# Layer 0's attention in 64-row score matmuls and split transposes, with the forget terms added by VectorE

## The chip, the cores and the metric

One core of a Trainium2 chip runs the whole program in one launch. The metric is the device time of an execution in microseconds, the median over the runs. The profile is that of one execution.

## The reference

Two decoder layers over 2048 positions of width 1024, batch 1. Each layer norms its input, scales and shifts it by a conditioning vector, mixes over positions and adds the gated, normed result.

Layer 0's mixer has two parts over one projection:

- FoX, 8 heads of 64: scores q.k/8 + (F[query] - F[key]) under the causal mask, where F is the running sum of log-forget gates of the head; softmax; times v; divided by the sum; gated by SiLU. F[query] is the same for all keys of a row and leaves the softmax as it is.
- Differential attention, 4 heads: two causal score maps with their own queries and keys of 64, two softmaxes p1 and p2, and (p1 - lam p2) v with v of 128 columns; then an RMSNorm and the gate.

Layer 1's mixer (dilated windows, 16 heads) is not touched but for where the code of its transposes stands.

All is float32 outside; scores are multiplied in parts, a high and a low one, in the type fp32r, as qh.kh + qh.kl + ql.kh.

## The kernel before

The stages follow each other: projections of layer 0 (to about 790 us), its attention (791 to 1600), its output projection, then the same for layer 1. A scheduler orders each engine's instructions by the order in which the program names them, the buffers at hand and its own estimate of costs.

`attention0` runs over pairs p of heads: 0 to 3 are four pairs of FoX heads, 4 to 7 the four differential heads with their two maps. Each p has two halves of eight units. A unit is a block of 128 queries, number i, against its i + 1 blocks of 128 keys. Half 0 alternates units of chunk 3 (i 12 to 15) and chunk 0 (i 0 to 3); half 1 those of chunk 2 and chunk 1. `run` takes the units in order. A unit's scores are put, piece by piece, into the groups of the unit three before it (AHEAD = 3).

- `scores`, one head (or map) at a time: for each piece of up to 512 keys two matmuls of 128 contraction rows into one bank of the tile `s` (three banks). Rows 0 to 63 and 64 to 127 of the key and query tiles hold different parts, so two matmuls give the three products; FoX's forget terms ride along as four extra rows (K1, K2, Q1, Q2 tiles, filled once with ones and zeros). DVE evicts each bank (L845, L848 with the causal mask `maskd` for the last piece) and takes the row minimum of the negated scores; ACT then does the exponential over the row in place (L853) and its sum.
- `combine` (differential only): DVE multiplies P1 by c1 and adds P0 (L883 to L885).
- `turn`, per group of 4 key blocks: `flip` transposes the blocks of 128 by 128 on TensorE (L701) into one bank of `t` (two banks) and copies it out as a tile `pt` (L704). FoX: ACT and DVE by turns; differential: ACT.
- `av`, one group later: probabilities times values into `o` (L919), FoX in 64-column halves for its two heads.
- `finish`: the divisors, for the differential heads the norm (L964 to L970; the product with the gate, L969, on POOL).

POOL is otherwise idle in this stage. Loads go through the SP queue, those before the first unit through POOL's. The last key tiles become room for the output weights: `WO_AT` says at which units six of eight are loaded, the other two are loaded in `out_proj`.

Layer 1's stage `dilated` has its two heads side by side in 64 rows each (L1256, three products), and transposes in two parts of 64 rows (L1283, copied out in L1288, its AV is L1305).

Of the kernel before, what the change touches and what calls it, by code (L numbers as in the profile page):

```python
# [8 lines left out]
F32 = mybir.dt.float32  # L9
F32R = mybir.dt.float32r  # L10
# [8 lines left out]
S, D = 2048, 1024  # L19
# [63 lines left out]
def trunk(ctx: ExitStack, tc: tile.TileContext, A, out):  # L83
# [42 lines left out]
    f_d = dram.tile([4, 8, S], F32R, name="fd")  # L126
# [376 lines left out]
    def forget():  # L503
# [27 lines left out]
        fh = fp.tile([128, 128], F32R, name="fh")  # L531
        fl = fp.tile([128, 128], F32R, name="fl")
        SC.copy(fh, ps[:, 256:384])
        V.tensor_tensor(fl, ps[:, 256:384], fh.bitcast(F32), OP.subtract)
        for part, x in ((0, fh), (1, fl)):
            dma(dap(f_d, part * 8 * S, [[128, 128], [1, 128]]), x)
            n = fp.tile([128, 128], F32R, name=f"fn{part}")
            V.tensor_scalar(n, x.bitcast(F32), -1.0, None, OP.mult)
            dma(dap(f_d, (2 + part) * 8 * S, [[128, 128], [1, 128]]), n)
# [87 lines left out]
    def first_rows(l, wo, ps_p, og, gh, gl, more=None):  # L627
# [8 lines left out]
        for e in range(len(wo)) if more is None else range(7):  # L636
            if more is not None:
                more(e)
# [58 lines left out]
    def flip(ap, aps, blocks, eng, bufs):  # L697

        ps = aps.tile([128, 512], F32, tag="t", name="t_ps", bufs=2)
        for j, b in enumerate(blocks):  # L700
            TE.transpose(ps[:, 128 * j:128 * j + 128], b, ident)  # L701
        n = 128 * len(blocks)
        pt = ap.tile([128, 512], F32, tag="pt", name="pt", bufs=bufs)
        last_flip[eng is SC] = SC.copy(pt[:, :n], ps[:, :n]) if eng is SC else V.tensor_copy(pt[:, :n], ps[:, :n])  # L704
        return pt
# [18 lines left out]
    P_BUFS = ((512, 4), (1024, 4), (2048, 4))  # L724
    HALVES = ((3, 0), (2, 1))

    def attention0():
# [8 lines left out]
        aps = pool(aps_es, "atps", 1, PS)  # L736

        def k_tile(j, n):
            K = kp.tile([128, S], F32R, name=f"K{n}_{j}")
            if n == 2:  # L740
                PO.memset(K[64:128, :].bitcast(F32), 1.0)
            return K

        Ks = [k_tile(j, n) for j in range(2) for n in (1, 2)]
        Q2s = [ap.tile([128, 512], F32R, name=f"Q2_{j}") for j in range(8)]

        def q_fill(eng, js):
            for j in js:
                eng.memset(Q2s[j][64:128, :].bitcast(F32), 0.0)
                eng.memset(Q2s[j][64:68, :].bitcast(F32), 1.0)  # L750

        q_fill(V, range(4))
        Q1s = [ap.tile([128, 512], F32R, name=f"Q1_{j}") for j in range(8)]
        M = 16 * 64 * S
        keys, queries, values, gates = {}, {}, {}, {}

        def load_k(p, j):
            h = 2 * (p % 4) + j
            if p >= 4:
                K = Ks[(h + 4) % 6]  # L760
                for a in (0, 1024):
                    dma2(K[:, a:a + 1024], qkd, (8 + h) * 64 * S + a, M, [[S, 64], [1, 1024]])
                keys[p, j] = K, K
                return
            K1, K2 = Ks[2 * (h % 3):2 * (h % 3) + 2]
            o = 64 * j * S
            for a in (0, 1024):
                dma2(K1[:, a:a + 1024], qk0[4 + p], o + a, 128 * S, [[S, 64], [1, 1024]])
                dma(K2[0:64, a:a + 1024], dap(qk0[4 + p], o + a, [[S, 64], [1, 1024]]))
                dma(K2[66:68, a:a + 1024], dap(f_d, h * S + a, [[8 * S, 2], [1, 1024]]))  # L770
            keys[p, j] = K1, K2

        def load_q(p, half, ns=(0, 1)):
            for n in ns:
                c = HALVES[half][n]
                for j in range(2):
                    h = 2 * (p % 4) + j
                    s = 4 * half + 2 * n + j
                    Q1, Q2 = Q1s[s], Q2s[s]
                    a = 512 * c  # L780
                    if p >= 4:
                        dma2(Q1, qkd, h * 64 * S + a, 0, [[S, 64], [1, 512]])
                        last = dma2(Q2, qkd, M + h * 64 * S + a, 0, [[S, 64], [1, 512]])
                    else:
                        o = 64 * j * S + a
                        dma2(Q1, qk0[p], o, 0, [[S, 64], [1, 512]])
                        dma(Q2[0:64], dap(qk0[p], 128 * S + o, [[S, 64], [1, 512]]))
                        last = dma(Q2[64:66], dap(f_d, (16 + h) * S + a, [[8 * S, 2], [1, 512]]))
                    queries[p, j, c] = Q1, Q2
            return last  # L790
# [9 lines left out]
        def loads_at(p, half):  # L800

            if half == 0:
                if 0 < p < 4:
                    load_k(p, 1)
                if p < 7:
                    load_k(p + 1, 0)
                if 3 <= p < 7:
                    load_k(p + 1, 1)
                load_q(p, 1)
            elif p < 7:  # L810
                load_q(p + 1, 0)
# [3 lines left out]
        load_k(0, 0)  # L815
        load_q(0, 0, (0,))
        dma(maskd, A["cst"][:, C_MD:C_MD + 512])
        load_k(0, 1)
# [3 lines left out]
        with tc.issue_after(last.ins):  # L822
            q_fill(PO, range(4, 8))
            Ks += [k_tile(2, n) for n in (1, 2)]
            rw = row_tiles(ap2, 2)

        def scores(d, j, p, i, l):
# [4 lines left out]
            m4 = ap.tile([128, 8], F32, tag="m4", name="m4", bufs=16)  # L832

            def piece(k):
                if k == 0:
                    d[j] = ap.tile([128, n0], F32, tag=f"P{n0}", name=f"P{n0}", bufs=bufs)
                P = d[j]
                c0, n = cl[k]
                ps = aps.tile([128, 512], F32, tag="s", name="s_ps", bufs=3)
                for a in range(2):  # L840
                    TE.matmul(ps[:, :n], queries[p, j, i // 4][a][:, 128 * (i % 4):128 * (i % 4) + 128],  # L841
                              keys[p, j][a][:, c0:c0 + n], start=a == 0, stop=a == 1)
                m = m4[:, k:k + 1]
                if k < len(cl) - 1:
                    V.tensor_scalar(P[:, c0:c0 + n], ps[:, :n], 0.0, 3.0e38, OP.add, OP.min, accum_out=m)  # L845
                    return
                u = min(n, W - c0)
                V.tensor_tensor_reduce(P[:, c0:c0 + u], ps[:, :u], maskd[:, 512 - u:512], 1.0, 3.0e38,  # L848
                                       OP.add, OP.min, m)
                if len(cl) > 1:  # L850
                    m = m4[:, 4:5]
# [608 lines left out]
```

## Time and profile before

| what | value |
|---|---|
| median of 3 runs | 3265.45 us (3259.69 to 3265.56) |
| the profiled execution | 3263.24 us, span 3261.5 us |
| TensorE matmul busy | 3149.6 us (97%), granted clock 0.982 |
| DVE, ACT, POOL busy | 1572.2, 1294.9, 427.8 us (48, 40, 13%) |
| layer 0's attention, FoX pairs | about 791 to 1250 us |
| layer 0's attention, differential heads | about 1250 to 1600 us |

Matmuls overlap, so a busy time near 100% does not say how much of it could go; the distance from one start to the next does. Times in a stage are to be read from that stage's windows, not from the page's totals.

### The profile page before, as it was taken

Reading aid. Unit: us, or ns where it says so; the run is one execution under the profiler, and the core shown is the slowest. Engines: PE = TensorE matmul, PEld = TensorE weight load, DVE = VectorE, ACT = ScalarE, POOL = GpSimd, SP = SyncE. Lnnn points to the kernel's source line nnn. Section 1 sums busy time; section 2 is a strip of 40 time slices with the busy share of each in tenths; the row PEclk is TensorE's granted clock in tenths of the full one; section 3 lists DMA queues with packets and bytes.
Section 4 is the critical chain, followed back from the end, with each engine's and each line's share of the span. In section 5 each row is a group of like instructions: output and inputs, shape, how many; then the busy total and the mean of one; then the engine's idle time right before and its main releaser. Section 6 shows DMA issues by size and latency. Waiting matters only on the chain. (4 is left out here: it accounts for less than half of the span.)

```text
span 3261.5 us, 56531 instructions
## 1 busy us (share of the span) xinstructions
PE 3149.6 (97%) x22044; PEld 2603.7 (80%) x22044; DVE 1572.2 (48%) x4180; ACT 1294.9 (40%) x2937; POOL 427.8 (13%) x404
## 2 busy tenths in 40 slices
PE   7999999999999999999999999999999899989898
PEld 6978889987777778888778998888888777767687
DVE  6443421002666668888663402311100677777743
ACT  5311111112555556777542321111111767676321
POOL 3200100003000000010032202220000022212422
PEclk8999999999999999999999999999999999998899
DMA  7255542217223324432342324674314554544252
GB/s 261 80 183 189 175 144 85 72 62 194 69 78 98 93 66 125 117 92 72 120 159 104 132 86 134 201 217 142 113 62 148 161 169 158 179 153 143 79 191 97
DMA packets 281812, 424.12 MB, mean 130 GB/s; under 512 B 32156, under 2 KB 160156, under 8 KB 276552
## 3 DMA queue, kind: packets, MB, share of 16 engines
q1 hardware_dynamic: 277496, 407.87, 40.1%
q0 software_dynamic: 4048, 12.64, 1.4%
q8 instruction: 173, 2.83, 0.4%
q14 instruction: 95, 0.78, 0.1%
HBM read 268.15 MB, written 152.25 MB: 129 GB/s over the span
## 5 line engine op out<-in xcount | busy, mean ns | idle before, releaser
L245 PE MATMUL pj<-hl,wh 128*128 128x512 f32 x1536 | 389.1, 395 | 0.0
L245 PE MATMUL pj<-hh,wh 128*128 128x512 f32 x1536 | 389.1, 395 | 0.0
L245 PE MATMUL pj<-hh,wl 128*128 128x512 f32 x1536 | 388.9, 395 | 0.0
L841 PE MATMUL s_ps<-K,Q 128*128 128x512 f32 (+2 forms) x1280 | 356.4, 391 | 8.6 <-DVE P L845 8.1
L245 PEld LDWEIGHTS pj<-hl,wh 128*128 128x128 f32 x1536 | 289.1, 188 | 68.9 <-issue 0.5
L245 PEld LDWEIGHTS pj<-hh,wl 128*128 128x128 f32 x1536 | 288.6, 188 | 68.3 <-issue 0.2
L853 ACT ACTIVATE P<-P,m 128x1664 f32<-128x1664 f32 (+15 forms) x256 | 307.2, 1201 | 89.9 <-DVE m L852 84.0
L245 PEld LDWEIGHTS pj<-hh,wh 128*128 128x128 f32 x1536 | 287.9, 188 | 68.3 <-issue 1.0
L919 PE MATMUL o_ps<-pt,v 128*64 128x128 f32 (+1 forms) x3264 | 335.6, 281 | 6.3 <-ACT pt L704 5.5
L919 PEld LDWEIGHTS o_ps<-pt,v 128*64 128x64 f32 (+1 forms) x3264 | 271.2, 155 | 69.3 <-issue 43.1
L1266 ACT ACTIVATE P<-P,st 128x256 f32<-128x256 f32 (+3 forms) x512 | 266.8, 523 | 107.5 <-DVE st L1264 106.7
L230 DVE TENSOR_TENSOR wl<-w,wh 128x512 fp32r<-128x512 f32 (+1 forms) x128 | 84.9, 705 | 404.9 <-ACT wh L229 404.9
L845 DVE TENSOR_SCALAR_CACHE_REDUCE P<-s_ps 128x512 f32<-128x512 f32 (+1 forms) x384 | 248.4, 667 | 64.8 <-PE s_ps L841 58.9
L701 PE MATMUL t_ps<-cc,P 128*128 128x128 f32 x1632 | 251.3, 278 | 4.0 <-DVE c L884 1.6
L1264 DVE CUSTOM_DVE_ANT_0 P<-s_ps,band 128x256 f32<-128x256 f32 (+3 forms) x512 | 204.2, 446 | 99.7 <-PE s_ps L1256 94.5
L841 PEld LDWEIGHTS s_ps<-K,Q 128*128 128x128 f32 x1280 | 209.0, 190 | 48.1 <-DVE P L845 16.7
L704 ACT COPY pt<-t_ps 128x512 f32<-128x512 f32 (+3 forms) x320 | 163.4, 517 | 197.9 <-PE t_ps L701 195.9
L1256 PE MATMUL s_ps<-K,Q 64*128 64x256 f32 (+2 forms) x1536 | 202.3, 334 | 24.7 <-DVE st L1264 23.3
L701 PEld LDWEIGHTS t_ps<-cc,P 128*128 128x128 f32 x1632 | 187.3, 142 | 39.1 <-issue 25.8
L266 ACT ACTIVATE hi<-pj 128x512 fp32r<-128x512 f32 x80 | 47.9, 598 | 348.7 <-PE pj L245 309.5
L1305 PE MATMUL o_ps<-pt,v 128*64 128x128 f32 x2272 | 179.6, 291 | 5.4 <-DMA v<-v 5.4
L1256 PEld LDWEIGHTS s_ps<-K,Q 64*128 64x128 f32 x1536 | 147.3, 197 | 46.1 <-DVE st L1264 34.9
(247 smaller groups left out, 4584.9 us busy)
## 6 DMA issues: line engine op xcount, KB each, us to landing
Q<-q SPq DMA_DIRECT2D x31, 1024.0 KB
ada<-ada_w SPq DMA_DIRECT2D x96, 256.0 KB
sg<-t2k SPq DMA_DIRECT2D x64, 256.0 KB
Q<-qkd SPq DMA_DIRECT2D x128, 128.0 KB
w<-w SPq DMA_DIRECT2D x64, 256.0 KB
xt<-x SPq DMA_DIRECT2D x32, 512.0 KB
q<-yb SPq DMA_DIRECT2D x64, 256.0 KB
x<-x SPq DMA_DIRECT2D x28, 512.0 KB
```

The source lines that it names most:

```text
L230: V.tensor_tensor(wl[:, 2 * q:2 * q + 2, :n], w[:, :, :n], wh[:, 2 * q:2 * q + 2, :n].bitcast(F32), OP.subtract)
L245: TE.matmul(ps, a[:, d, 128 * j:128 * j + 128], b[:, d, :], start=n == 0, stop=n == 23)
L701: TE.transpose(ps[:, 128 * j:128 * j + 128], b, ident)
L704: last_flip[eng is SC] = SC.copy(pt[:, :n], ps[:, :n]) if eng is SC else V.tensor_copy(pt[:, :n], ps[:, :n])
L841: TE.matmul(ps[:, :n], queries[p, j, i // 4][a][:, 128 * (i % 4):128 * (i % 4) + 128], keys[p, j][a][:, c0:c0 + n], start=a == 0, stop=a == 1)
L845: V.tensor_scalar(P[:, c0:c0 + n], ps[:, :n], 0.0, 3.0e38, OP.add, OP.min, accum_out=m)
L853: SC.activation(P[:, :W], P[:, :W], AF.Exp, bias=m, scale=-1.0, accum_out=l)
L919: TE.matmul(o[:, cs], values[p][:, g + b, hs], pts[g, j][:, 128 * b:128 * b + 128], start=g + b == 0, stop=g + b == i)
L1256: TE.matmul(ps[hh][:, o:o + N], q[hs, qs], t["keys"](kk[hs]), start=k == 0, stop=k == 2)
L1264: V.tensor_tensor_reduce(P[:, hh, j, :n], ps[hh][:, o:o + n], m[:, m.shape[1] - n:], 1.0, 3.0e38, OP.add, OP.min, mn)
L1266: SC.activation(P[:, hh, j, :n], P[:, hh, j, :n], AF.Exp, bias=mn, scale=-1.0, accum_out=l)
L1305: TE.matmul(to, values[p, br][:, kc, hs], where[hh, j, o, kc], start=k == 0, stop=k == n - 1)
```

## The change

Layer 0's attention takes the form that layer 1's has:

- Keys and queries of the two heads (or maps) of a p lie in rows 0 to 63 and 64 to 127 of common tiles; the high and low parts are separate tiles. A piece is scored for both heads at once: three products, each as two matmuls of 64 rows, into two of the three `s` banks.
- FoX's forget terms no longer ride in the matmul. F is loaded to all 128 partitions (`load_f`) and added by DVE in the pass that evicts a bank; for the last piece POOL first adds it to the mask. `forget` writes F once, as float32.
- `flip` turns up to 8 blocks as pairs of 64-row halves into both `t` banks; two copies follow, one in three of them on DVE, the others on ACT. It is one function for both layers; layer 1's transposes are as they were.
- A group has 8 (head, block) pairs: four key blocks of two FoX heads as before, eight key blocks for a differential head. PT_BUFS is 3 tiles of double size.
- `combine` runs on POOL, as a multiplication and an addition, for units with k % 4 < 2 (i 12, 14, 0, 2, 8, 10, 4, 6).
- Rows up to 512 columns no longer have tiles of their own. Keys and forget terms have four tiles each; the forget tiles and key tiles become the output weights' room, and all eight are loaded before `out_proj` (`first_rows` goes over eight).

```diff
-            m4 = ap.tile([128, 8], F32, tag="m4", name="m4", bufs=16)
+            m4 = ap.tile([128, 2, 8], F32, tag="m4", name="m4", bufs=6)
...
-                ps = aps.tile([128, 512], F32, tag="s", name="s_ps", bufs=3)
-                for a in range(2):
-                    TE.matmul(ps[:, :n], queries[p, j, i // 4][a][:, 128 * (i % 4):128 * (i % 4) + 128],
-                              keys[p, j][a][:, c0:c0 + n], start=a == 0, stop=a == 1)
-                m = m4[:, k:k + 1]
-                if k < len(cl) - 1:
-                    V.tensor_scalar(P[:, c0:c0 + n], ps[:, :n], 0.0, 3.0e38, OP.add, OP.min, accum_out=m)
-                    return
...
+                if k == len(cl) - 1 and p < 4:
+                    for j in range(2):
+                        masks[j] = ap.tile([128, 512], F32, tag="fm", name="fm", bufs=4)
+                        PO.tensor_tensor(masks[j][:, 512 - u:], forgets[p][j][:, c0:c0 + u], maskd[:, 512 - u:], OP.add)
+                ps = [aps.tile([128, 512], F32, tag="s", name="s_ps", bufs=3) for _ in range(2)]
+                for a, b, first in ((0, 0, True), (0, 1, False), (1, 0, False)):
+                    for j in range(2):
+                        hs = slice(64 * j, 64 * j + 64)
+                        TE.matmul(ps[j][:, :n], queries[p, i // 4][hs, a, qs], keys[p][b][hs, c0:c0 + n],
+                                  start=first, stop=a == 1)
+                for j in range(2):
+                    P, m = d[j], m4[:, j, k:k + 1]
+                    if k < len(cl) - 1:
+                        if p < 4:
+                            V.tensor_tensor_reduce(P[:, c0:c0 + n], ps[j][:, :n], forgets[p][j][:, c0:c0 + n], 1.0, 3.0e38,
+                                                   OP.add, OP.min, m)
+                        else:
+                            V.tensor_scalar(P[:, c0:c0 + n], ps[j][:, :n], 0.0, 3.0e38, OP.add, OP.min, accum_out=m)
+                        continue
+                    V.tensor_tensor_reduce(P[:, c0:c0 + u], ps[j][:, :u], masks[j][:, 512 - u:512], 1.0, 3.0e38,
+                                           OP.add, OP.min, m)
...
-                V.scalar_tensor_tensor(d[0][:, :W], d[1][:, :W], c1, d[0][:, :W], OP.mult, OP.add)
+                if k % 4 < 2:
+                    PO.tensor_scalar(d[1][:, :W], d[1][:, :W], c1, None, OP.mult)
+                    PO.tensor_tensor(d[0][:, :W], d[1][:, :W], d[0][:, :W], OP.add)
+                else:
+                    V.scalar_tensor_tensor(d[0][:, :W], d[1][:, :W], c1, d[0][:, :W], OP.mult, OP.add)
...
-            pieces += head_pieces(0) + head_pieces(1)
+            pieces += [first] + [lambda n=n: box["f"][n]() for n in range(1, len(chunks(W)))]
...
-            nh = 2 if fox else 1
+            nh, step = (2, 4) if fox else (1, 8)
...
-                n = min(4, i + 1 - g)
-                for j in range(nh):
+                engs = []
+                for _ in range(2):
                     count[0] += 1
-                    eng = V if fox and count[0] % 2 == 0 else SC
...
+                    engs.append(V if count[0] % 3 == 0 else SC)
+                blocks = [(j, g + b) for b in range(min(step, i + 1 - g)) for j in range(nh)]
```

The new `flip`, the loads of keys, forget terms and queries, and the buffers:

```python
    def flip(ap, aps, blocks, engs, bufs):
        ps = [aps.tile([128, 8, 64], F32, tag="t", name="t_ps", bufs=2) for _ in range(2)]
        for n, b in enumerate(blocks):
            for k in range(2):
                rs = slice(64 * k, 64 * k + 64)
                TE.transpose(ps[k][:, n], b[rs], ident[rs, rs])
        pt = ap.tile([128, 8, 128], F32, tag="pt", name="pt", bufs=bufs)
        for k, eng in enumerate(engs):
            f = SC.copy if eng is SC else V.tensor_copy
            last_flip[eng is SC] = f(pt[:, :len(blocks), 64 * k:64 * k + 64], ps[k][:, :len(blocks)])
        return [pt[:, n] for n in range(len(blocks))]
...
        def load_k(p, cuts=(0, 1024, 2048)):
            keys[p] = K = [big(1) for _ in range(2)]
            for a, b in zip(cuts[:-1], cuts[1:]):
                for part in range(2):
                    t, step = qk(p, 1, part)
                    dma(K[part][:, a:b], dap(t, step * part + a, [[S, 128], [1, b - a]]))
        def load_f(p, cuts=(0, 1024, 2048)):
            forgets[p] = F = [big(0).bitcast(F32) for _ in range(2)]
            for j in range(2):
                for a, b in zip(cuts[:-1], cuts[1:]):
                    dma(F[j][:, a:b], dap(f_d, (2 * p + j) * S + a, [[0, 128], [1, b - a]]))
```

```diff
-    P_BUFS = ((512, 4), (1024, 4), (2048, 4))
+    P_BUFS = ((1024, 4), (2048, 4))
...
-    AHEAD, PT_BUFS = 3, 6
+    AHEAD, PT_BUFS = 3, 3
```

## Rows read from the trace of the kernel before

**Rows 1.** Windows, FoX and differential half: us, busy PE PEld DVE ACT POOL, clock, DMA

```profile
791.00:1250.00 459.00, 456.05 (x3935) 350.00 (x3935) 312.25 (x980) 246.33 (x434) 0.11 (x1) 1.00 0.35 95
1250.00:1600.00 350.00, 333.96 (x2323) 296.86 (x2323) 298.52 (x937) 261.76 (x488) 24.93 (x15) 0.99 0.31 90
```

**Rows 2.** Waits of the FoX half: us in total, times, longest

```profile
PEld o_ps L919 <- issue: 42.6, 161, 0.4
```

**Rows 3.** Waits of the differential half, the same columns

```profile
PEld o_ps L919 <- ACT pt L704: 12.5, 20, 2.6
...
PEld o_ps L919 <- issue: 0.5, 2, 0.2
```

**Rows 4.** Groups by form over the whole execution: busy us, mean ns

```profile
L701 PE MATMUL t_ps<-cc,P 128*128 128x128 f32 x1632 | 251.3, 278 | 4.0 <-DVE c L884 1.6 <-ACT P L853 1.4 <-DVE c L883 0.8
L845 DVE TENSOR_SCALAR_CACHE_REDUCE P<-s_ps 128x512 f32<-128x512 f32 x336 | 223.2, 683 | 63.0 <-PE s_ps L841 57.2 <-PE t_ps L701 5.0
...
L704 DVE COPY pt<-t_ps 128x512 f32<-128x512 f32 x112 | 77.3, 690 | 75.3 <-PE t_ps L701 74.2
```

**Rows 5.** Timeline of TensorE, FoX half: start us, us, what, how many

```profile
1036.75 0.61 PE L841 MATMUL s_ps<-K,Q 128*128 128x384 f32 x2
1037.30 0.43 PE L919 MATMUL o_ps<-pt,v 128*64 128x128 f32 x2
...
1038.42 0.71 PE L841 MATMUL s_ps<-K,Q 128*128 128x512 f32 x2
1038.97 0.27 PE L701 MATMUL t_ps<-cc,P 128*128 128x128 f32 x1
...
1039.58 0.60 PE L841 MATMUL s_ps<-K,Q 128*128 128x384 f32 x2
1040.01 0.49 PE L701 MATMUL t_ps<-cc,P 128*128 128x128 f32 x3
...
1116.19 1.09 PE L701 MATMUL t_ps<-cc,P 128*128 128x128 f32 x8
1117.04 1.52 PE L841 MATMUL s_ps<-K,Q 128*128 128x512 f32 x6
1118.49 0.65 PE L919 MATMUL o_ps<-pt,v 128*64 128x128 f32 x6
```

**Rows 6.** Timeline of TensorE in layer 1's attention, the same columns

```profile
2700.24 0.71 PE L1283 MATMUL t_ps<-cc,P 64*128 64x64 f32 x16
2700.76 1.64 PE L1256 MATMUL s_ps<-K,Q 64*128 64x512 f32 x9
2702.32 0.43 PE L1305 MATMUL o_ps<-pt,v 128*64 128x128 f32 x2
2702.90 0.97 PE L1256 MATMUL s_ps<-K,Q 64*128 64x512 f32 x3
2703.80 1.52 PE L1305 MATMUL o_ps<-pt,v 128*64 128x128 f32 x22
```

**Rows 7.** Timeline of the differential half: combinations, first transposes after them, an exponential

```profile
1419.22 1.95 DVE L885 SCALAR_TENSOR_TENSOR P<-P,c,P 128x1664 f32<-128x1664 f32 x1
...
1423.59 0.27 PE L701 MATMUL t_ps<-cc,P 128*128 128x128 f32 x1
...
1440.31 2.22 DVE L885 SCALAR_TENSOR_TENSOR P<-P,c,P 128x1920 f32<-128x1920 f32 x1
1440.41 3.25 POOL L969 TENSOR_TENSOR sq<-sq,sg 128x512 f32<-128x512 f32 x1 [42.06 <-ACT sq L968]
...
1446.83 0.38 PE L701 MATMUL t_ps<-cc,P 128*128 128x128 f32 x2
...
1448.83 2.01 ACT L853 ACTIVATE P<-P,m 128x2048 f32<-128x2048 f32 x1
```

**Rows 8.** Groups by form over the whole execution: POOL's 512-wide passes

```profile
L1379 POOL TENSOR_TENSOR or<-or 128x512 f32<-128x512 f32 x31 | 40.0, 1292 | 154.7 <-DVE or L1373 154.7
...
L273 POOL COPY yb<-lo 128x512 f32<-128x512 f32 x32 | 22.2, 694 | 5.3 <-DVE lo L267 5.2
```

More of the change, by code (lines that the diff above doesn't have):

```diff
@@ L530, in forget @@
         TE.transpose(ps[:, 256:384], F.rearrange("p h t -> p (h t)"), ident)
[L531 to L539, printed above, removed]
+        fT = fp.tile([128, 128], F32, name="fT")
+        V.tensor_copy(fT, ps[:, 256:384])
+        dma(dap(f_d, 0, [[128, 128], [1, 128]]), fT)
         es.close()
@@ L625, in trunk, with first_rows @@
     Y_BUFS, BUILD_AT = 7, 5
-    def first_rows(l, wo, ps_p, og, gh, gl, more=None):
+    def first_rows(l, wo, ps_p, og, gh, gl, more, n):
         og, gh, gl = [[x.rearrange("p (e n) -> p e n", n=128) for x in t] for t in (og, gh, gl)]
@@ L635, in first_rows @@
                 V.tensor_tensor(gl[r], og[r], gh[r].bitcast(F32), OP.subtract)
-        for e in range(len(wo)) if more is None else range(7):
-            if more is not None:
-                more(e)
+        for e in range(n):
+            more(e)
             for r in range(2):
@@ L695, in trunk @@
     last_flip = {}
[L697 to L705, printed above, removed]
+    def flip(ap, aps, blocks, engs, bufs):
+        ps = [aps.tile([128, 8, 64], F32, tag="t", name="t_ps", bufs=2) for _ in range(2)]
+        for n, b in enumerate(blocks):
+            for k in range(2):
+                rs = slice(64 * k, 64 * k + 64)
+                TE.transpose(ps[k][:, n], b[rs], ident[rs, rs])
+        pt = ap.tile([128, 8, 128], F32, tag="pt", name="pt", bufs=bufs)
+        for k, eng in enumerate(engs):
+            f = SC.copy if eng is SC else V.tensor_copy
+            last_flip[eng is SC] = f(pt[:, :len(blocks), 64 * k:64 * k + 64], ps[k][:, :len(blocks)])
+        return [pt[:, n] for n in range(len(blocks))]
     def to_rows(ap, ps, x, n, rd, k, w):
@@ L752, in attention0 @@
[L752 to L763, printed above, removed]
-                return
[L765 to L771, printed above, removed]
+        keys, queries, forgets, values, gates, wo = {}, {}, {}, {}, {}, []
@@ L775, in load_q @@
                 c = HALVES[half][n]
[L776 to L789, printed above, removed]
+                queries[p, c] = Q = ap.tile([128, 2, 512], F32R, tag="Q", name="Q", bufs=4)
+                t, step = qk(p, 0, 0)
+                last = dma(Q, dap(t, 512 * c, [[S, 128], [step, 2], [1, 512]]))
             return last
@@ L822, in attention0, with scores @@
         with tc.issue_after(last.ins):
-            q_fill(PO, range(4, 8))
-            Ks += [k_tile(2, n) for n in (1, 2)]
             rw = row_tiles(ap2, 2)
-        def scores(d, j, p, i, l):
+        def scores(d, p, i, lt, col):
             W = 128 * (i + 1)
@@ L870, in start @@
                     lts[p, half] = ap2.tile([128, 2, 8], F32, tag="lt", name="lt", bufs=3)
-            def head_pieces(j):
-                box = {}
-                def first():
-                    box["f"] = scores(d, j, p, i, lts[p, half][:, j, col:col + 1])
-                    box["f"][0]()
-                return [first] + [lambda n=n: box["f"][n]() for n in range(1, len(chunks(W)))]
             def combine():
@@ L915, in av @@
                 cs = slice(128 * (i % 4), 128 * (i % 4) + 128)
-                for b in range(min(4, i + 1 - g)):
+                for b in range(g, min(g + step, i + 1)):
                     for j in range(nh):
                         o, hs = (O[64 * j:64 * j + 64], slice(64 * j, 64 * j + 64)) if fox else (O, slice(0, 128))
-                        TE.matmul(o[:, cs], values[p][:, g + b, hs], pts[g, j][:, 128 * b:128 * b + 128],
-                                  start=g + b == 0, stop=g + b == i)
-                if i % 4 == 3 and g + 4 > i:
+                        TE.matmul(o[:, cs], values[p][:, b, hs], pts[j, b], start=b == 0, stop=b == i)
+                if i % 4 == 3 and g + step > i:
                     cs = slice(512 * c, 512 * c + 512)
@@ L928, in av, with split_raw @@
                         SC.copy(ogs[p][:, cs], O)
-            gs = range(0, i + 1, 4)
+            gs = range(0, i + 1, step)
             tail = finish(p, half) if k == 7 else []
-            return {AHEAD: pieces}, [(lambda g=g: turn(g), lambda g=g: av(g), tail if g + 4 > i else []) for g in gs]
+            return {AHEAD: pieces}, [(lambda g=g: turn(g), lambda g=g: av(g), tail if g + step > i else []) for g in gs]
+        def split_raw(e):
+            wo.append(big(e // 4))
+            split_wo(raws[0][:, e % 2], wo[e])
         def finish(p, half):
@@ L957, in chunk @@
                     og = gates[p]
-                    TE.matmul(x, sels[0], r, start=True, stop=True)
+                    TE.matmul(x, sels[0][0:64], r[0:64], start=True, stop=True)
                     V.tensor_tensor(og[:, cs], x, og[:, cs], OP.mult)
```

98 lines of the change are left out of this document (46 added, 52 removed).

## The prediction

> **What bounds the kernel now.** I read the stage windows first, then the waits of the two halves of layer 0's attention, the groups by form for durations, and last stretches of the timeline for what one operation costs TensorE. The attention stage is the only one whose instructions change in number. In its forgetting half (FoX, 459 us) TensorE is busy 456.1 us while DVE has 312.3, ACT 246.3 and POOL 0.1; in its differential half (350 us) TensorE has 334.0, DVE 298.5, ACT 261.8 and POOL 24.9 [rows 1]. The reader is to see that the first half ends with TensorE alone, and that in the second DVE stands at 85%, so TensorE can give little there before DVE decides. The clock is at its upper level in both (1.00 and 0.99). The sum below is therefore one of TensorE time. A matmul's duration does not tell that time, since matmuls overlap; I take start to next start from the timeline.
>
> Waits point the same way. In the first half weight loads for the AV matmuls stand idle 42.6 us in 161 places without a releaser, one for each of the 160 groups in which probabilities are turned and multiplied; in the second half, 2 places and 0.5 us [rows 2, 3]. AV there is 128 by 64 in the first half, 128 by 128 in the second, and scores and transposes are 128 by 128 in both: the idle time belongs to a change of the array's shape.
>
> **The change, part by part.**
>
> *Transposes.* Eight 128 by 128 transposes take from 1116.19 to 1117.04, 0.85 us [rows 5]. Layer 1 already turns blocks in two halves of 64: sixteen halves go from 2700.24 to 2700.76, 0.52 us [rows 6]. That is 0.106 against 0.065 us a block, 0.041 saved. There are 1632 blocks [rows 4], two thirds of them FoX: -45 us in FoX and -22 in the second half. Bounds: -67 if groups stay whole; half of it, -33, if the planner breaks groups up and leaves single halves.
>
> *Shape changes.* After the change scores and transposes are 64 by 128 and AV of the second half stays 128 by 128, so it pays what FoX pays now. Two 384-column score matmuls before an AV take 0.55 us (1036.75 to 1037.30), before a transpose 0.43 (1039.58 to 1040.01) [rows 5]: 0.12 to enter. I take the same to leave, 0.24 a visit. With groups of eight blocks there are 24 groups to a head, 96 in all: +23 us. Bounds: 96 x 0.12 = 12, and 160 x 0.24 = 38 if as many visits remain as there are groups now. FoX pays this already and keeps its 160.
>
> *Scores.* A piece (two heads, up to 512 keys) is four 128-row matmuls before and six 64-row ones after; if the two heads run side by side they take three slots. Whether they do hangs on PSUM: there are three score banks, a piece wants two. Layer 1 shows both outcomes in one place. Nine 64-row matmuls run from 2700.76 to 2702.32, 1.56 us: three pairs and then three of one head alone; the other head's three follow at 2702.90 and take 0.90, AV between [rows 6]. So a piece that finds two banks costs about 0.85 with the shape change behind it, and one split in two costs some 0.7 and 0.9. Before, six matmuls take 1.45 (1117.04 to 1118.49) and a lone two 0.55 before a transpose, so 0.67 before AV [rows 5].
>
> Where do pieces come in a burst? Each small unit of half 0 (one group) carries the four pieces of the large unit three ahead. Evictions give a bank back every 0.683 us and an accumulator read [rows 4], about as long as one head's three matmuls alone, so the second piece is split as layer 1 shows. For the third and fourth no row decides; I take half split, half paired. FoX, per large unit of 512-wide pieces: before 1.45 + 5 x 0.60 = 4.45; after 1.56 + 0.85 + half of (4 x 0.85 + 2 x 0.85) = 4.96, where 0.60 and 0.85 stand for followers of both kinds. +0.51, x 0.9 for narrower pieces, x 16 units: +7. Pieces that stand alone save some 0.2 (0.97 for four of such six before, about 0.75 after, with the mean width); FoX has 64: -13. Sixteen bursts of two cost +0.36 x 0.85: +5. FoX together: -1. In the second half a lone two costs only 0.55, and units have half the groups, so bursts are longer: large units +0.50 x 0.9 x 16 = +7; 16 single pieces -3; 16 bursts of three, 2.98 before and 3.40 after, x 0.85: +6; 16 of two, 1.88 and 2.22, x 0.7: +4. Together +14. Bounds for both halves: all pieces paired, 320 pieces at some -0.22 (0.3 for a 512-wide one, x 0.75 for width): -72; every later piece split: +42 in place of my +13.
>
> *Forget terms.* FoX evictions add the term from SBUF in the pass that already takes the minimum. The masked pass of the last piece does just that today, and layer 0's plain 512-column pass takes 0.683 [rows 4]; I take no difference. POOL adds term and mask, two 512-wide adds a unit at 1.29 [rows 8], 64 units: 165 us at most on an engine with 0.1 us of work in 459 [rows 1]. If that cover failed, the last eviction of a unit would wait up to 2.6 us, 64 times, but the operands are there a pair of heads ahead. Loads: 2 MB more of forget terms a pair of heads, less keys and queries, one way or the other under a DMA share of 0.35 [rows 1]. Start of the stage: 0 to +5 us if the terms land late; I take 0. The smaller forget() and the wo tiles' new place lie beside busy TensorE stretches: 0, bounds -3 to +3.
>
> *Copies and waits.* DVE takes a third of the copies in place of half in FoX (160 to 107) and none in the rest: -53 x 0.69 = -37 us on DVE in FoX [rows 4], about as much more in the second half, where POOL takes over combinations worth about as much. So DVE keeps its 298.5 us there. AV waits 12.5 us for ACT's copies [rows 3]; with two engines I take half back: -6.
>
> *Combination on POOL.* For half the units P1 x c + P0 goes to POOL in two passes. DVE does 1920 columns in 2.22 us. POOL: an add of 512 takes 1.29, a one-input copy 0.69 [rows 8]; x 3.75 gives 7.4, so 5.2 longer. And both heads' scores now end together, so the second exponential (2.01 us at full width) starts when the first ends. Room: the 1920-column combination ends at 1442.53 and its first transpose starts at 1446.83, 4.3 later; at 1664 columns 1421.17 and 1423.59, 2.4 [rows 7]. 5.2 less these is 0.9 and 2.8, x 4 pairs: +15. Bounds: 0 (TensorE fills with later scores) and +68, below.
>
> **Sum**: -45 - 22 + 23 - 1 + 14 - 6 + 15 = -22. The profiled execution took 3263.24 us with a span of 3261.5; 3239.5 + 1.7 = 3241.2. Its time is 2.2 under the median of the three runs, within their spread, so 3241 stands as it is.
>
> **The rivals.** *All pieces paired.* Scores give -72 in place of +13: 3241 - 85 = 3156. For it: FoX's TensorE hardly waits for banks, so by the time it comes to a piece two may be free. Against it: layer 1's split runs, and DVE's 298.5 us in the second half, a floor. The Trainium skill, TensorEngine Tiling (Array Packing), PSUM Bottleneck, says the same against it: tiling speeds TensorE but not PSUM's evacuation. By that rule the second half's part of the 85, about half, falls away: 3198. The trace agrees in that half, with DVE at 85% [rows 1].
>
> *POOL late: slower.* In the second half POOL also does the gate product L969, 1.29 us for such a form elsewhere but 3.25 beside DVE's 1920-column combination, which ran at its usual 2.22 [rows 7, 8]: POOL waits, DVE does not. If each of POOL's passes loses 1.95 so, and the serial exponentials add 1.9, a POOL combination is 11 us later, 6.7 and 8.6 over its room, and a DVE one at the widest units 1.7: 17 us a pair, 68 in all, in place of 15: 3294. It decides from about 5.6 us of lateness on, the room plus what TensorE can do meanwhile. Against it: TensorE has scores for later units then, if banks are free. The Trainium skill, SBUF — State Buffer, SBUF: two separate sides, has a lock as the cause: DVE and POOL take the shared ports for a whole instruction. By that rule only DVE's own combinations (two SBUF inputs) block POOL, and evictions do not. The trace agrees as far as the one 3.25 shows.
>
> *No gain.* If transposes come in fragments (-33 in place of -67) and TensorE hides POOL's lateness (0 in place of 15), the rest as above: 3241 + 34 - 15 = 3260, no change that can be told. For it: FoX's transposes come in runs of one to three already [rows 5].
>
> **How the numbers follow.** The forecast has 0.43, with its own range 3220 to 3258 (transposes' and switches' bounds, half of the bursts'). Paired 0.18, POOL late 0.28, no gain 0.11. A difference under 0.2% (6.5 us) is about what measurement can't tell from none. Faster: 0.40 of the forecast's and 0.18, 0.58; same: 0.03 and 0.09, 0.12; slower 0.30. The range for 8 in 10 takes in most of the paired and the late case: 3160 to 3300.
>
> **What would show it.** Transposes: pairs starting together, 0.06 us apart, eight blocks in about 0.5 us. Scores: runs of six or nine and lone threes; a lone three in most bursts is my step, none is the first rival. Shape changes: idle weight loads before AV in the second half, some 96 places. POOL: first transposes of the 1664- and 1920-column units that wait for POOL; more than 5 us each is the second rival. FoX should shorten by 40 to 50 us and the second half lengthen by up to 25. I am wrong if FoX doesn't shorten, or if DVE, not TensorE, ends the second half's waits.

## The result and the profile after

The changed kernel takes 3397.31 us (median of 4 runs, 3393.84 to 3402.51) against 3265.51 for the kernel before on the same chip: a ratio of 1.0406, 95% interval 1.0387 to 1.0425. The prediction said 3241, with a range of 3160 to 3300.

The profiled execution spans 3391.7 us, 130.2 more than before. I cut layer 0's attention into two stretches by the starts of its transposes: from the first of all to the first of the differential heads, and from there to the end of the last AV. Before they took 452.1 and 348.4 us, after 458.6 and 469.5. So 6.5 us of the loss lie in FoX, 121.1 in the differential half, 2.6 elsewhere.

Windows of the kernel after, FoX and differential half, columns as in [rows 1]:

```profile
791.00:1258.00 467.00, 436.54 (x5357) 335.80 (x5357) 283.76 (x925) 261.60 (x486) 122.97 (x130) 0.97 0.24 80
1258.00:1729.00 471.00, 404.32 (x3170) 313.07 (x3166) 334.33 (x975) 241.91 (x463) 174.25 (x72) 0.90 0.18 57
```

In FoX TensorE's busy time did fall, from 456.1 us [rows 1] to 436.5, but its idle time rose from 3 to 30 us. In the differential half it is idle 67 us (16 before), and the granted clock averages 0.90 in place of 0.99. The waits of that half after (us in total, times, longest) name the place:

```profile
PEld s_ps L822 <- DVE P L831: 72.1, 39, 7.8
PE s_ps L822 <- DVE P L831: 56.8, 20, 7.6
DVE og L961 <- POOL sq L960: 52.3, 12, 5.5
```

TensorE waits for score banks, that is, for DVE's evictions (L831); and DVE waits for POOL's gate product (L960, L969 before). One such place in the timeline of the kernel after:

```profile
1390.78 5.12 POOL L863 TENSOR_SCALAR P<-P,c 128x1920 f32<-128x1920 f32 x1 [16.33 <-ACT sq L958]
...
1394.60 0.94 PE L822 MATMUL s_ps<-K,Q 64*128 64x512 f32 x6
...
1395.87 1.27 POOL L960 TENSOR_TENSOR sq<-sq,sg 128x512 f32<-128x512 f32 x1
...
1397.09 4.23 POOL L864 TENSOR_TENSOR P<-P,P 128x1920 f32<-128x1920 f32 x1
1397.17 4.70 DVE L961 SCALAR_TENSOR_TENSOR og<-og,subl,sq 128x512 f32<-128x512 f32 x1 [4.28 <-POOL sq L960]
...
1401.87 0.67 DVE L831 TENSOR_SCALAR_CACHE_REDUCE P<-s_ps 128x512 f32<-128x512 f32 x1
...
1402.60 2.38 PE L822 MATMUL s_ps<-K,Q 64*128 64x512 f32 x6 [7.06 <-DVE P L831]
```

POOL multiplies a row of 1920 columns (5.12 us); the gate product stands behind it. DVE's next instruction is L961, which needs the gate: DVE waits 4.28 us. By then POOL has begun its second pass, and L961, two of whose inputs lie in SBUF, takes 4.70 us in place of 0.75 and ends half a microsecond after that pass. The evictions queued behind it resume at 1401.87, and TensorE's scores have waited 7.06 us. Then the clock:

```profile
1394.00:1402.00 8.00, 1.53 (x14) 0.81 (x12) 4.83 (x3) 1.44 (x4) 7.32 (x3) 0.86 0.00 0
1402.00:1412.00 10.00, 8.09 (x30) 5.87 (x32) 5.37 (x18) 1.02 (x1) 3.48 (x3) 0.50 0.22 67
```

After eight us in which TensorE was busy for 1.53, the next ten are granted 0.50 of full speed, the lower level of 1.2 GHz. The stall is paid twice, as waiting and then as slower matmuls.

TensorE's time by kind of work, summed from each start to the next, so waits are included (us; worked out from the starts of all matmuls of a stretch):

| stretch, kernel | transposes | scores | AV | finish |
|---|---|---|---|---|
| FoX, before | 121.4 | 163.9 | 161.0 | 5.7 |
| FoX, after | 115.7 | 184.7 | 155.0 | 2.9 |
| differential, before | 58.7 | 146.2 | 127.7 | 15.6 |
| differential, after | 69.3 | 207.1 | 172.4 | 20.4 |
| differential, split transposes alone (e4) | 72.1 | 156.2 | 138.1 | 15.6 |
| differential, after without the blocking (e9) | 58.5 | 164.7 | 158.7 | 20.1 |

### The profile page after: what moved, and what is told of

Read it like the earlier page. It is cut to its first block, busy times and chain, and to the rows that moved or that the text cites. A ratio compares the mean times of both kernels' runs of the same rounds, so it can differ in the third digit from the quotient of the medians.

```text
span 3391.7 us, 61048 instructions
## 1 busy us (share of the span) xinstructions
PE 3203.1 (94%) x24316; PEld 2608.4 (77%) x24316; DVE 1570.9 (46%) x4144; ACT 1286.9 (38%) x2954; POOL 680.2 (20%) x559
## 5 line engine op out<-in xcount | busy, mean ns | idle before, releaser
L822 PE MATMUL s_ps<-K,Q 64*128 64x512 f32 (+2 forms) x1920 | 375.4, 405 | 62.9 <-DVE P L831 56.8
L697 PEld LDWEIGHTS t_ps<-cc,P 64*128 64x128 f32 x5536 | 277.1, 144 | 144.0 <-ACT pt L701 51.7
L697 PE MATMUL t_ps<-cc,P 64*128 64x64 f32 x5536 | 349.6, 238 | 39.7 <-ACT pt L701 31.6
L822 PEld LDWEIGHTS s_ps<-K,Q 64*128 64x128 f32 x1920 | 238.4, 195 | 122.2 <-DVE P L831 73.4
L701 DVE COPY pt<-t_ps 128x512 f32<-128x512 f32 (+5 forms) x384 | 231.0, 612 | 192.1 <-PE t_ps L697 155.7
L907 PEld LDWEIGHTS o_ps<-pt,v 128*64 128x64 f32 (+1 forms) x3264 | 262.8, 161 | 64.3 <-issue 43.8
L701 ACT COPY pt<-t_ps 128x512 f32<-128x512 f32 (+7 forms) x448 | 215.0, 497 | 245.3 <-PE t_ps L697 236.4
L1249 PEld LDWEIGHTS s_ps<-K,Q 64*128 64x128 f32 x1536 | 148.5, 200 | 43.9 <-DVE st L1257 33.9
```

What stands on the lines that cost most here:

```text
L697: TE.transpose(ps[k][:, n], b[rs], ident[rs, rs])
L701: last_flip[eng is SC] = f(pt[:, :len(blocks), 64 * k:64 * k + 64], ps[k][:, :len(blocks)])
L822: TE.matmul(ps[j][:, :n], queries[p, i // 4][hs, a, qs], keys[p][b][hs, c0:c0 + n], start=first, stop=a == 1)
L907: TE.matmul(o[:, cs], values[p][:, b, hs], pts[j, b], start=b == 0, stop=b == i)
L1249: TE.matmul(ps[hh][:, o:o + N], q[hs, qs], t["keys"](kk[hs]), start=k == 0, stop=k == 2)
```

## The experiments

Stretches in us as defined above, from one profiled execution each; a time without a ratio is one run. The kernel before, run beside them, has medians of 3261 to 3267, and single runs of it lie between 3257 and 3271. How far a stretch strays by itself can be read where its code is the same: FoX takes 457.5 to 459.9 us in the kernel after, e1, e3 and e9, and 451.8 to 453.8 in the kernel before, e2 and e10.

| run | FoX | differential | time | ratio to before |
|---|---|---|---|---|
| before | 452.1 | 348.4 | 3265.5 | 1 |
| after | 458.6 | 469.5 | 3397.3 | 1.0406 |
| e1, combinations on DVE | 457.9 | 407.5 | 3329.9 | 1.0214 [1.0191, 1.0238] |
| e2, before + POOL's combinations | 453.8 | 426.8 | 3351.3 | |
| e3, gate product on DVE | 459.9 | 445.1 | 3370.8 | |
| e4, split transposes alone | 451.2 | 382.3 | 3301.7 | 1.0121 [1.0099, 1.0142] |
| e5, 64-row scores alone | 468.2 | 413.7 | 3354.8 | |
| e6, e1 in the program's order | 509.6 | 447.0 | 3424.1 | |
| e7, e1 with four score banks | 454.2 | 393.0 | 3310.0 | |
| e8, e1 with copies by turns | 453.0 | 401.5 | 3321.5 | |
| e9, after without the blocking | 457.5 | 401.9 | 3338.0 | |
| e10, e2 without the blocking | 451.8 | 369.3 | 3294.2 | 1.0092 [1.0073, 1.0110] |
| e11, before, FoX's transposes split | 448.7 | 348.1 | 3260.9 | 0.9996 [0.9981, 1.0010] |
| e12, the same in pairs 1 to 3 alone | 444.4 | 348.0 | 3256.4 | 0.9975 [0.9962, 0.9988] |
| e13, e7 and e8 together | 452.4 | 403.2 | 3330.7 | |

### POOL's combination: e1, e2, e3, e9, e10

**e1.** In `combine`:

```diff
-                if k % 4 < 2:
-                    PO.tensor_scalar(d[1][:, :W], d[1][:, :W], c1, None, OP.mult)
-                    PO.tensor_tensor(d[0][:, :W], d[1][:, :W], d[0][:, :W], OP.add)
-                else:
-                    V.scalar_tensor_tensor(d[0][:, :W], d[1][:, :W], c1, d[0][:, :W], OP.mult, OP.add)
+                V.scalar_tensor_tensor(d[0][:, :W], d[1][:, :W], c1, d[0][:, :W], OP.mult, OP.add)
```

> The changed kernel with every combination P1 x c + P0 of the second half on DVE, in one pass, none on POOL. Theory T1 (POOL's two passes of a combination hold up the gate product that is queued behind them; DVE's next product waits for the gate, and DVE's in-order queue with every score eviction waits with it): the second half falls from 469 us to 335 to 365, the whole to 3260 to 3290. Rival T2 (TensorE itself lost it: split pieces, more shape changes, a lower clock): the second half stays above 440, the whole at 3370 to 3400. Rival T3 (both heads' exponentials end late together, so the combination is late wherever it is made): the second half 410 to 470, the whole 3340 to 3400. In all of them the first half stays at 455 to 462.

62 us of the 121 go, half of what T1 forecast: POOL's combination is the largest single cause, and there is a second one of 59 us.

**e2.** The same lines put into the kernel before, the other way round.

> The kernel before with one edit: in half of the units of the second half the combination is made on POOL in two passes, as in the changed kernel. T1 (POOL's combination alone does the harm): the second half goes from 349 us to 430 to 460, the whole to 3345 to 3380. T2 and T3 (scores, transposes or the paired exponentials do it): under 15 us more, 3260 to 3280.

78 us more in the second half, 3 short of T1's range, and the whole within it: T1. Neither paired scores nor split transposes are needed for the harm.

**e3.** `V.tensor_tensor(sq, sq, gates[p][:, cs], OP.mult)` for every pair, in place of POOL for all but the last.

> The changed kernel with the gate product of the second half on DVE for every pair, so that no DVE instruction waits for POOL's queue; the combinations stay on POOL. T1 as stated (the wait for the gate is most of it, about 52 us of waits and what follows): 50 to 90 us off the changed kernel's 3397, so 3305 to 3345. If it is the passes on POOL by themselves (a late combination, or DVE slowed while POOL runs): under 25 us off. T2, T3: no change, within 10 us.

Only 26.5 us off the time, just over the 25 of the second theory: the wait for the gate is not most of it. DVE's groups by form of e3 in the differential half (busy us, mean ns) show what remains:

```profile
L831 DVE TENSOR_SCALAR_CACHE_REDUCE P<-s_ps 128x512 f32<-128x512 f32 x158 | 102.3, 682 | 14.8 <-PE s_ps L822 14.2 <-PE t_ps L697 0.2
L861 DVE SCALAR_TENSOR_TENSOR c<-c,nlam,lt 128x1 f32<-128x1 f32 x62 | 45.9, 740 | 1.0
L960 DVE TENSOR_TENSOR sq<-sq,sg 128x512 f32<-128x512 f32 x14 | 26.4, 1887 | 2.9 <-ACT sq L959 2.9
```

L861 works on one column. Beside no POOL pass it takes 0.214 us in the mean (47 of the 62, worked out from the timeline); the 7 that ran into POOL's addition, L864, took 2.9 to 3.6 us, and ended with that pass (by 0.02 us in the median). Of the 8 that met the multiplication, L863, seven took 1.05 to 2.5 us and ended 0.2 to 1.5 us before it did; the eighth, begun 3.2 us into a pass of 4.5, took 0.22. L960 is slowed the same way, to 1.89 us in the mean. Evictions, which read PSUM, take 0.682 as ever.

**e9** takes those inputs away, and with them the gate product from POOL's queue. The combinations stay on POOL:

```diff
-                V.scalar_tensor_tensor(c1, c1, nlam, lt[:, 0, col:col + 1], OP.mult, OP.mult)
+                V.tensor_scalar(c1, lt[:, 0, col:col + 1], c1, nlam, OP.mult, OP.mult)
...
-                    SC.activation(sq, sq, AF.Exp, scale=-0.5)
-                    (V if p == 7 else PO).tensor_tensor(sq, sq, gates[p][:, cs], OP.mult)
-                    V.scalar_tensor_tensor(og[:, cs], og[:, cs], subl, sq, OP.mult, OP.mult)
+                    SC.activation(x, sq, AF.Exp, scale=-0.5)
+                    V.tensor_tensor(x, x, gates[p][:, cs], OP.mult)
+                    V.scalar_tensor_tensor(og[:, cs], og[:, cs], subl, x, OP.mult, OP.mult)
```

> The changed kernel, combinations on POOL as they are, with three edits that leave no short DVE instruction with two tensor inputs in SBUF: c1 is made with two column scalars, and the exponential of the finish is written to its PSUM bank, from where DVE takes the gate product (no longer on POOL) and the final product. Theory L (a DVE instruction with two SBUF inputs stands still while a POOL pass runs, and all evictions queue behind it; instructions with an input in PSUM do not): these instructions take their usual 0.2 and 0.7 us, the second half falls from 469 us to 390 to 415, the whole to 3310 to 3345. Rival T3 (the combination on POOL is simply late, 9.4 us at 1920 columns): second half 440 or more. If the instruction with two column scalars still waits for POOL, in between.

```profile
L861 DVE TENSOR_SCALAR c<-lt,c,nlam 128x1 f32<-128x1 f32 x62 | 16.8, 270 | 0.9
...
L961 DVE SCALAR_TENSOR_TENSOR og<-og,subl,bc_ps 128x512 f32<-128x512 f32 x14 | 10.4, 744 | 0.1
...
L960 DVE TENSOR_TENSOR bc_ps<-bc_ps,sg 128x512 f32<-128x512 f32 x14 | 9.8, 697 | 6.6 <-ACT bc_ps L959 6.6
```

```profile
1262.00:1665.00 403.00, 382.57 (x3168) 296.61 (x3164) 305.73 (x987) 242.91 (x461) 158.86 (x61) 1.00 0.22 67
```

In these groups of e9 nothing is slowed, though every one of the 28 wide ones ran beside a POOL pass. The differential half loses 67.6 us, and its clock is 1.00 again (the window above). That is theory L, with both of its ranges met: what DVE lost beside POOL's passes, and not the lateness of the combination, was the cost. T3 falls. But e9 takes away two things at once, the wait for the gate behind POOL's passes and the slowed instructions; e3, which takes away the first and leaves the second, gains 24.4 us of the 67.6 in this half.

**e10.** The edits of e9 in e2.

> The kernel before with combinations on POOL in half of the units and the same three edits. Theory L: of the 79 us that POOL's combinations added to the second half of the kernel before, nearly all go: second half 345 to 365 us, the whole 3260 to 3285. If moving work off DVE is worth something by itself (DVE stands at 85% there): 340 to 347, the whole 3253 to 3262. Rival T3 (late combination): second half 380 or more, the whole 3295 or more.

58 of e2's 78 us go. The 21 left are 4 over the range, and the waits of e10's differential half say what they are:

```profile
PEld t_ps L701 <- POOL P L887: 28.6, 12, 7.0
PE t_ps L701 <- POOL P L887: 26.4, 10, 6.8
```

Here the transposes do wait for a late combination. That is the prediction's own mechanism, at 21 us against its 15, though in the kernel before. Why the wait is 26.4 us there and 4 to 8 in the changed kernel and e9 was not tested.

### Transposes and scores: e4 and e5

**e4.** The kernel before with `flip`, `turn`, `av` and PT_BUFS of the changed one. **e5.** e1 with those of the kernel before (layer 1 keeps its own).

> The kernel before with one part of the change alone: transposes in two parts of 64 queries, groups of eight blocks, one copy for each part (a third of them on DVE), three buffers for the turned blocks; scores, forget terms and combinations as before. By the prediction's terms (transposes -67, shape changes of the second half +23, half the waits of AV -6): 3215 to 3225. Rival (what the shorter transposes save goes to waits for the copies, of which both parts' banks must come free): 3255 to 3275; and if the fragments cost more than before, above that.

> The changed kernel with all combinations on DVE and with whole 128 by 128 transposes as in the kernel before (groups of four, one copy each): of the change only the 64-row scores with the added forget terms remain. It completes a square with the kernel before, the run with split transposes alone and the run with both. Theory S (a change between 64 and 128 rows costs some 0.09 us going in and 0.09 to 0.17 coming out, and one is now paid at each of about 200 runs of scores): first half 465 to 490 us, second half 405 to 435, so neither part is cheap alone. Rival (it is the split transposes that cost, the scores gain): first half 435 to 452, second half 345 to 375.

Both forecasts of a gain fell: e4 is even above its rival's range, and e5 came out as theory S said in both halves. Four kernels, before, e4, e5 and e1, make a square in the differential half: 348.4 before, 382.3 with split transposes, 413.7 with 64-row scores, 407.5 with both. The two losses don't add. The reading that fits is that a border costs, a step on TensorE between a matmul of 64 rows and one of 128, and that with both parts in 64 rows only AV has borders. e4's TensorE shows the borders at the transposes:

```profile
1461.81 0.34 PE L704 MATMUL t_ps<-cc,P 64*128 64x64 f32 x2
1462.08 0.96 PE L845 MATMUL s_ps<-K,Q 128*128 128x512 f32 x3
1462.97 0.33 PE L704 MATMUL t_ps<-cc,P 64*128 64x64 f32 x2
1463.23 0.96 PE L845 MATMUL s_ps<-K,Q 128*128 128x512 f32 x3
```

Two halves, one block, take 0.26 to 0.27 us to the next start. In e4's differential half a block inside a run of transposes costs 0.061 us by the median (two halves 3 ns apart), the first step of a run 0.11, the last 0.152. Before, a block costs 0.11 and the step to a score 0.028. There are 189 runs in e4 of 2.9 blocks, 187 of 2.9 before: 382 against 314 ns a run. At this length the split form loses.

Borders at AV, in e9 (first two lines) and in the kernel before, on TensorE's timeline:

```profile
1475.32 0.49 PE L907 MATMUL o_ps<-pt,v 128*128 128x128 f32 x2
1475.73 0.95 PE L822 MATMUL s_ps<-K,Q 64*128 64x512 f32 x3
```

```profile
1425.20 0.39 PE L919 MATMUL o_ps<-pt,v 128*128 128x128 f32 x2
1425.34 0.48 PE L841 MATMUL s_ps<-K,Q 128*128 128x256 f32 x2
```

The same two matmuls take 0.41 us to the next start against 0.14. A visit is a run of AV matmuls between other work. By medians of the differential half in e9 and before: a 512-column score before AV 323 and 232 ns, the first AV matmul to the second 213 and 109, the last to a transpose 206 and 112, to a score 205 and 31, a transpose to AV 152 and 109. With the counts in e9 (92, 133, 79, 43 and 40) that is 39 us for 133 visits, 0.29 each. The Trainium skill, TensorEngine Tiling (Array Packing), Key Properties, says that a change of tiling mode drains TensorE; it gives no price, and these are this case's.

### Banks and order: e6, e7, e8, e13

**e6.** Each piece, each group of transposes and each group of AV in a block of this kind, on top of e1 (`pe` holds the last matmul of each block, and the next block may not be issued before it):

```diff
+            with tc.issue_after(pe[-1].ins):
+                return f()
```

> The changed kernel with all combinations on DVE and with TensorE held to the order in which the program names its work in layer 0's attention: whole groups of transposes, whole pieces of six score matmuls, whole groups of AV, none cut by the planner. Theory F (cut groups and lone halves ate what the 64-row form saves): first half 380 to 435 us in place of 458, second half 345 to 390 in place of 407. Rival W (the cuts only fill waits for banks and copies that TensorE would otherwise spend idle): first half 450 or more, second half 405 or more, with more idle time of TensorE before transposes and scores.

The rival, W, and by far: both halves are 40 to 52 us longer than e1's, the clock 0.91 and 0.92. Waits of e6 over the stage:

```profile
PEld t_ps L697 <- ACT pt L701: 74.6, 59, 3.5
PE t_ps L697 <- ACT pt L701: 62.4, 50, 3.3
...
PEld s_ps L822 <- DVE P L832: 47.2, 60, 3.2
```

The cuts that I had taken for waste fill waits for the two banks of the transposes and the three of the scores.

**e7.** Four score banks, on top of e1 (finish's products move to the tag `t`):

```diff
-                ps = [aps.tile([128, 512], F32, tag="s", name="s_ps", bufs=3) for _ in range(2)]
+                pp = aps.tile([128, 2, 512], F32, tag="s", name="s_ps", bufs=2)
+                ps = [pp[:, j] for j in range(2)]
```

> The changed kernel with all combinations on DVE and four score banks in place of three, as two pairs, so that a piece always finds both of its banks (the small products of the finish take turns in the banks of the transposes to make room). Theory B (three banks are why pieces are split and the scores save nothing): score runs of six by pairs, no lone threes; first half 420 to 445 us in place of 458, second half 370 to 395 in place of 407. Rival (a pair's two banks come free together and later, so TensorE waits as long): first half 450 to 465, second half 400 to 415.

FoX gains 3.7 (the rival), the second half 14.5 (theory B). The share of score matmuls that start in pairs rises there from 31% in e1 to 62%, not to all. In FoX the scores' own time falls by 10 us (184.5 in e1, 174.4), but TensorE waits longer for ACT's copies (31.3 us in place of 23.4).

**e8.** On top of e1, `engs = [SC, V] if fox else [SC, SC]`.

> The changed kernel with all combinations on DVE and, in the first half, one copy of each group of transposes on ACT and the other on DVE (in place of two on ACT or one of each, by a count of three); in the second half both on ACT. Theory C (the two parts' banks come free one ACT copy after another, and TensorE waits for them, some 60 us of waits by weight loads and matmuls together in the first half): first half 440 to 452 us in place of 458. Rival (DVE's score evictions come later by as much): first half 456 to 470. Second half within 8 us of 407.

FoX gains 4.9 and lies between the two; the second half gains 6, within its 8. Theory C's mechanism is not what the trace shows: in FoX TensorE waits 22.8 us for ACT's copies, as in e1 (23.4).

**e13.** e7 and e8 together.

> The changed kernel with all combinations on DVE, four score banks as two pairs, and in the first half one copy on ACT and one on DVE. If bank shortage is what hides the first half's gain and the two add: first half 458 - 4 - 5 = 449 us or less, down to 440; second half 385 to 395. Rival (each only moves the wait to the other): first half 453 to 458. Either way the second half stays over 380, since changes of shape around about 120 to 140 runs of AV remain, and the whole at 3295 to 3310, slower than before.

FoX 452.4, close to the rival: the gains don't add, and TensorE waits 30.2 us for ACT's copies, as in e7. The second half missed its range (403.2; the clock was 0.96), as did the whole, which is 21 us over e7. Why the two together lose there stays open.

### The part that pays: e11 and e12

**e11** splits the transposes of FoX alone, in the kernel before; **e12** keeps whole ones in pair 0 too:

```diff
-                if not fox:
+                if p == 0 or not fox:
```

> The kernel before with transposes in two parts of 64 queries in the first half alone; second half as before, its transposes whole. From the run with split transposes in both halves, whose second, third and fourth pairs took 109.5 to 110.1 us in place of 112.3: 2.3 us off each pair, so first half 443 to 452 us, second half 346 to 352, the whole 3253 to 3265. Rival (the granted clock falls at the start of the stage as in that run, whose first pair lost 6 us): first half 451, the whole within 5 us of before.

> The kernel before with transposes in two parts of 64 queries in the second, third and fourth pair of the first half alone; the first pair and the second half keep whole transposes. From the run with the whole first half split: those three pairs 109.5 to 110.1 us in place of 112.2, the first pair 115 to 116 as in the kernel before (there 119.0 when split, with the clock at 0.81 in its first 30 us). First half 443 to 447 us in place of 452, the whole 3252 to 3260, a ratio of 0.997 to 0.999. Rival (the clock's fall at the start is not caused by the split transposes, or moves to the second pair): no change, 0.999 to 1.001.

In e11 pairs 1 to 3 take 109.5 to 110.1 us in place of 112.3 and 112.1, but pair 0 takes 119.0 in place of 115.4, its first 30 us at a clock of 0.81 (1.00 before). The whole can't be told from the kernel before. In e12 pair 0 takes 115.0, its first 30 us at 0.94, and the forecast of its time holds. That the split transposes lower the clock there is not shown: in e11 it is at 0.96 already in the 27 us ahead of the first transpose, with the same code as before. e12's FoX half and a piece of TensorE's timeline in it:

```profile
791.00:1242.00 451.00, 448.47 (x4756) 335.88 (x4756) 294.80 (x942) 263.83 (x473) 0.00 (x0) 1.00 0.36 98
```

```profile
1101.44 1.09 PE L945 MATMUL o_ps<-pt,v 128*64 128x128 f32 x16
1102.46 0.71 PE L713 MATMUL t_ps<-cc,P 64*128 64x64 f32 x16
1103.11 1.20 PE L854 MATMUL s_ps<-K,Q 128*128 128x512 f32 x4
```

A whole group of sixteen halves takes 0.65 us to the next start where eight whole blocks took 0.85 [rows 5]. e12 is faster than the kernel before by 0.25% (interval 0.12 to 0.38%).

## Why the prediction was wrong

It forecast 22 us less; the span grew by 130. Point by point:

- **Combination on POOL** is the step that failed: it put the cost on DVE at nothing. It was priced at +15 for lateness, and the rival *POOL late* at 68, with the sentence "POOL waits, DVE does not". One row was read in one direction: there DVE's instruction had begun first [rows 7]. The same trace has the other direction:

```profile
1312.30 1.29 POOL L969 TENSOR_TENSOR sq<-sq,sg 128x512 f32<-128x512 f32 x1 [2.62 <-ACT sq L968]
1312.41 1.20 DVE L884 SCALAR_TENSOR_TENSOR c<-c,nlam,lt 128x1 f32<-128x1 f32 x1
```

Here POOL began first, and DVE's instruction on one column, 0.214 us elsewhere, ended with POOL's. e3 shows it at full size: of two that meet, the later one waits. The step cost 62 (e1) to 68 us (e9), through DVE's queue; first transposes wait for POOL only some 4 us in the changed kernel. The rival's 68 is that number by luck, and not by its mechanism. The Trainium skill, SBUF — State Buffer, Who interferes with whom, has it in a sentence: "Issue order, not op shape, decides who blocks." The runs agree where both inputs lie in SBUF: 0.214 us became 2.9 to 3.6 on one column.

- **POOL's one-input pass** was sized from a copy of 512 columns, 0.69 [rows 8]. At 1920 columns it takes 5.12 us, the two-input pass 4.23: 9.35 for both against 7.4. The error is small beside the queue's.
- **Transposes**, -45 and -22: -5.7 in FoX, and -0.2 in the second half once the blocking is out (e9). The price of a block in layer 1's run of eight was laid on 1632 blocks, but in the changed kernel they come in runs of 4.5 in FoX and 3.1 in the second half, and in FoX some 840 of 2176 halves start alone, each taking the slot of a pair. *No gain* had this term at half; it was less.
- **Scores**, -1 and +14: +20.8 and +18.5 (e9). The step saw split pieces and was right in kind for the second half. In FoX the shortage of banks is about half of the miss, as far as e7 shows (10 us less with four); the rest stays open. The rival *All pieces paired* is out: 39% of FoX's score matmuls after start in pairs.
- **Shape changes**, +23: the price of 0.24 a visit was near (0.29); the visits were 133, not 96, since groups are cut. 39 us (e9).
- **Forget terms**: 0. The eviction bears it out: with the added term, 512 wide, it takes 0.69 us beside 0.683 [rows 4]. No run takes the terms by themselves.
- **FoX shortens by 40 to 50 us**: it lengthened by 6.5. Busy time fell by 19.5, idle time rose by 27.5, and the clock was 0.97 in place of 1.00 (0.83 in the stage's first 30 us). The larger part of the idle time is TensorE's wait for ACT's copies, 23.6 us, and 0.2 before. FoX's waits in the kernel after:

```profile
PEld t_ps L697 <- ACT pt L701: 37.8, 45, 2.4
...
PE t_ps L697 <- ACT pt L701: 23.6, 35, 1.9
```

The same wait in the kernel before:

```profile
PE t_ps L701 <- ACT pt L704: 0.2, 1, 0.2
```

- **What would make it wrong** was named: FoX not shortening, and DVE ending the second half's waits. Both came.

Adding up the second half: 121.1 is 67.6 for what DVE lost beside POOL's passes (with the clock) and 53.5 without it; those are AV +31.0, scores +18.5, transposes -0.2, finish's products +4.5, within rounding.

## What to carry to other kernels

Before work is moved to POOL, list what DVE does meanwhile with two SBUF inputs, down to one-column instructions, and what is queued behind it; in e9 an input in PSUM kept DVE clear. Price a shorter matmul form by the run lengths that the scheduler really leaves, with one cost going in and one coming out, and move only those users whose neighbours already pay the border. When TensorE gets faster, the banks must come free faster too: in FoX here the saved busy time came back as idle time, at a lower clock.

## What was not expected of the hardware

- A DVE instruction on a single column took up to 3.6 us beside a POOL pass (0.214 alone), with both inputs in SBUF; the same product with column scalars took 0.27 there and elsewhere, and 512 columns with an input in PSUM 0.70 and 0.74 in all 28 cases beside a pass (e9).
- A lone transpose of 64 rows takes the same 0.06 us slot as two that start 3 ns apart.
- A multiplication by a column scalar is dearer on POOL than an addition of two tensors: 5.12 against 4.23 us at 1920 columns, 3.30 against 2.64 at 1152.
- Leaving 128-row AV for 64-row scores costs 0.17 us more than for 128-row ones (205 against 31 ns, e9 and before).
- A pass of POOL's multiplication let DVE's waiting instruction end 0.2 to 1.5 us before the pass itself ended; beside a pass of its addition the instruction ended with the pass (e3).
